# A two-block transformer kernel: the Silu of a condition vector moved, three coefficient rows made at another point of the program

## The chip, the cores and the metric

The kernel runs on one core of a Trainium2 chip. Its time is the device time of one execution in microseconds (us); the number compared is the median of several executions. The engines of the core are PE (matrix multiply; PEld loads its weights), DVE (element-wise work on vectors), ACT (functions, copies, casts), POOL (here it only sets constants and issues transfers) and SP (it only issues transfers).

## What is computed

An activation of 256 rows by 1024 columns passes through two blocks. The first block is one mLSTM mixer (an attention-like recurrence with 4 heads, forward and backward in time) and a gated feed-forward with a convolution. The second has two layers, each of feed-forward, mixer, feed-forward; the mixers are a gated linear attention (GLA) and a latent attention (MLA). Every sub-layer is modulated by vectors that come out of a condition vector:

```
mod = silu(c) @ w_mod + b_mod
sh1, sc1, ga1, sh2, sc2, ga2 = split(mod, 6)
hx = modulate(x, g_mix, sh1, sc1)
y  = mlstm_mixer(hx, ...)
x  = x + ga1 * y
hx = modulate(x, g_ffn, sh2, sc2)
x  = x + ga2 * conv_glu(hx, ...)
```

The second block does the same with its own condition vector `c_2`. A vector such as `ga1` multiplies the mixer's output column by column, so with the 256 rows on the partitions it is wanted as a *row*: 1024 numbers, the same on all 128 partitions.

## The kernel before

Activations lie in two tiles of 128 rows. Every weight is streamed from DRAM by SP in pieces of 128 x 1024 (512 KB) through a few `raw` buffers; ACT casts a piece to a high part (`whi`, L236), DVE subtracts to get the low part (`wlo`, L237), and each product is three matmuls (L250 to L252). "A projection" below is one of these matmuls of 512 columns.

The products of a condition vector with its weights are done on DVE while the other engines work on the main path: for each 128 outputs one piece of weight is loaded to `raw` and one instruction of DVE (`ttr`, L256) multiplies it with the condition row and sums. They stand in a list, `bg_queue`; `site()` takes as many from its front as a table says (`FILL`), and `need(keys)` takes from it until the named ones are done. The condition row is 128 x 1024, `c1` for the first block and `c2` for the second, which share one buffer (tag `crow`), so `c2` can't be written before the last `ttr` with `c1` has read it. `c2()` makes the row where it is first asked for: SP sends `c_2` from DRAM to all partitions (L158) and ACT applies Silu to all 128 x 1024 (L159).

`row_of(v)` turns a vector that lies as 128 x 8 into a row: PE transposes it (`rowp`, L389) into the one PSUM buffer of tag `tr`, ACT copies it out (`s8`, L391), POOL writes it to DRAM (`d<-s`, L393) and sends it back to all partitions (`row<-d`, L395). The same PSUM buffer `tr` holds `mp` of the mLSTM attention.

The mLSTM mixer first makes q, k, v and the output gate o (`as_proj`, four groups of 1024 columns; the gate's Sigmoid is L696). Then `attend(t, h)` runs for 2 row tiles x 4 heads: PE makes the scores (L706) and spreads the gate sums over the partitions (`mp`, L710), DVE and ACT turn them into weights (L716, Exp at L719 and L720, products at L722 to L725), PE multiplies them with the values (L733), and DVE and ACT normalise (L735 to L744). Then `wo_proj` is the output projection; its last step multiplies with the row `ga1` (L761). GLA and MLA have the same shape, and their last step multiplies with a row in `post2` (L921).

The order of instructions on each engine is the scheduler's: it goes by the order of the program, except that `urgent(offset)` lifts work by that many places. Attention runs under `urgent(300)` for the first tile and `urgent(2000)` for the second, so its instructions are put ahead of things written earlier, if what they need is there.

Of the kernel before, what the change touches and what calls it, by code (L numbers as in the profile page):

```python
# [7 lines left out]
F32 = mybir.dt.float32  # L8
# [3 lines left out]
AF = mybir.ActivationFunctionType  # L12
# [4 lines left out]
D = 1024  # L17
# [93 lines left out]
def kernel(ctx: ExitStack, tc: tile.TileContext, a: dict, out: bass.AP):  # L111
    nc = tc.nc
    V, S, T, G = nc.vector, nc.scalar, nc.tensor, nc.gpsimd
# [9 lines left out]
    row_p = pool("row", 2)  # L123
# [3 lines left out]
    sm = pool("sm", 4)  # L127
    dr = pool("dr", 2, space=bass.MemoryType.DRAM)
# [24 lines left out]
    def col(name, i=0, n=None):  # L153
        off, tot = COLS[name]
        return cols[:, off + i:off + i + (tot if n is None else n)]

    def load_act_row(src, dst):
        nc.sync.dma_start(out=dst, in_=src.partition_broadcast(128))  # L158
        S.activation(out=dst, in_=dst, func=AF.Silu)  # L159

    cc = ar.tile([128, D], F32, name="cc", tag="Q")
    c1 = row_p.tile([128, D], F32, name="c1", tag="crow", bufs=1)
# [106 lines left out]
    def site():  # L269
        bg(filler.pop(0))  # L270

    def need(*keys):
        while not done.issuperset(keys):
            bg()
# [17 lines left out]
    def scale1(dst, g):  # L292
        V.scalar_tensor_tensor(out=dst, in0=dst, scalar=1.0, in1=g, op0=ALU.add, op1=ALU.mult)
# [92 lines left out]
    def row_of(c):  # L386

        p = ps_tr.tile([8, 128], F32, name="rowp", tag="tr")
        T.transpose(p, c, ident)  # L389
        s8 = sm.tile([8, 128], F32, name="s8", tag="s8", bufs=2)  # L390
        S.copy(s8, p)  # L391
        d = dr.tile([8, 128], F32, name="d", tag="d")
        G.dma_start(out=d, in_=s8)  # L393
        r = row_p.tile([128, D], F32, name="row", tag="row")
        G.dma_start(out=r, in_=d.rearrange("a b -> (a b)").partition_broadcast(128))  # L395
        return r

    def row_load(src):
        r = row_p.tile([128, D], F32, name="row", tag="row")
        G.dma_start(out=r[:, :src.shape[-1]], in_=src.partition_broadcast(128))  # L400
        return r
# [40 lines left out]

    vec2 = []

    def c2():
        if not vec2:
            v = row_p.tile([128, D], F32, name="c2", tag="crow", bufs=1)
            load_act_row(a["c_2"], v)
            vec2.append(v)
        return vec2[0]  # L450

    for i, fin in ((2, None), (3, None), (4, "g_ffn"), (5, None)):
        dst = mod1[:, i, :]
# [153 lines left out]
    def mlstm():  # L607
# [94 lines left out]
        def attend(t, h):  # L702
# [40 lines left out]
            dst = so[:, t, h * 256:h * 256 + 256]  # L743
            V.scalar_tensor_tensor(out=dst, in0=hs, scalar=r, in1=dst, op0=ALU.mult, op1=ALU.mult)  # L744

        for t in range(2):
            with urgent(2000 if t else 300):
                for h in range(H):
                    attend(t, h)
                t_hilo(so[:, t, :], t)  # L750
            site()

    mlstm()
    need(("m", 2), ("m", 3), ("m", 4))
    ga1 = row_of(mod1[:, 2, :])

    def fin_mix(t, acc):
        y = wk.tile([128, D], F32, name="y", tag="xn")
# [250 lines left out]
    def gla():  # L1009
# [8 lines left out]
        rt = scratch(1).rearrange("p (t n) -> p t n", t=2)  # L1018
        gout = hp.tile([128, 256], F32, name="gout", tag="gout", bufs=1)
        G.dma_start(out=gout, in_=a["gl_gout"].partition_broadcast(128))  # L1020
        units, got = {}, {}

        def vr(i, t):
# [60 lines left out]
        with urgent():  # L1084
# [20 lines left out]
            for t in range(2):  # L1105
# [34 lines left out]
                    dst = rt[:, t, h * 256:h * 256 + 256]  # L1140
                    V.scalar_tensor_tensor(out=dst, in0=po, scalar=r, in1=dst, op0=ALU.mult, op1=ALU.mult)
                t_hilo(rt[:, t, :], t)
        need(5, 6, 7)
        coef = row_of(mod2[:, 5, :])

        def fin(t, acc):
            post2(coef, t, acc)
# [101 lines left out]
    def mla_mix():  # L1249
        scale = 192.0 ** -0.5  # L1250
        msk = hp.tile([128, 256], F32, name="amsk", tag="gout", bufs=1)
        G.dma_start(out=msk, in_=a["amask"])
        gq = row_load(a["mla_gq"])
        def attend(t, h):
            rp = slice((h % 2) * 64, (h % 2) * 64 + 64)
            n = 128 * (t + 1)
# [76 lines left out]
        for step in MLA_STEPS:  # L1333
            steps[step[0]](*[int(x) for x in step[1:]])
            site()
        need(14, 15, 16)
        coef = row_of(mod2[:, 14, :])

        def fin(t, acc):
            post2(coef, t, acc)  # L1340
# [162 lines left out]
```

## Time and profile before

| | us |
|---|---|
| median of 3 executions | 1430.35 |
| lowest, highest | 1429.79, 1434.51 |
| the profiled execution, its own time | 1434.38 |
| its span in the trace | 1432.6 |

The span is what the trace shows from the first to the last instruction; 1.8 us of the profiled execution's time lie outside it. Its mean granted clock of PE is 0.986 of full speed. In the page, busy time is the time in which an engine has an instruction running; a row of the timeline has, in brackets, how long the engine had been idle before the instruction, and what it was waiting for.

### The profile page before, as it was taken

How to read it: one execution, taken by the hardware profiler on the slowest of the kernel's cores; microseconds unless marked ns; L12 is line 12 of the kernel's file. 1: busy time of each engine (PE TensorE's matmuls, PEld its weight loads, DVE VectorE, ACT ScalarE, POOL GpSimd, SP SyncE). 2: the span in 40 equal slices, each digit the busy share in tenths (PEclk: the TensorE clock that was granted, in tenths of full speed). 3: DMA queues.
4: the chain of work that ended last, by engine and by line, in shares of the span. 5: the costliest groups of instructions: out<-in, count | busy, mean ns of one | idle time of the engine just before them, and what ended most of it. 6: DMA issues, size and time to landing. Idle time of an engine off the chain costs nothing.

```text
span 1432.6 us, 22526 instructions
## 1 busy us (share of the span) xinstructions
PE 1380.0 (96%) x8425; PEld 1204.0 (84%) x8425; DVE 1113.9 (78%) x2115; ACT 720.5 (50%) x1188; POOL 18.2 (1%) x42
## 2 busy tenths in 40 slices
PE   6999999999989999999999999999999999899997
PEld 6978877899978999878678999879999776789996
DVE  6887788898688888689788888698878786756563
ACT  4634764545354545566454545554554666644451
POOL 1000000000000000000000000000000000000000
PEclk8999999999999999999999999999999999999999
DMA  8576446797528999568548999469889472366750
GB/s 330 203 265 234 162 151 234 264 323 272 184 96 290 336 340 345 196 222 290 187 154 289 341 335 344 147 202 334 317 310 333 138 253 80 121 198 205 276 170 30
DMA packets 94943, 340.24 MB, mean 238 GB/s; under 512 B 10928, under 2 KB 11248, under 8 KB 94832
## 3 DMA queue, kind: packets, MB, share of 16 engines
q1 hardware_dynamic: 92736, 332.47, 65.6%
q0 software_dynamic: 2096, 6.33, 1.5%
q8 instruction: 66, 1.08, 0.3%
q14 instruction: 45, 0.37, 0.1%
HBM read 337.67 MB, written 1.08 MB: 236 GB/s over the span
## 4 chain that ended last, share of the span: by engine, by line
PE 70%; DVE 11%; DMA 10%; ACT 4%; issue 3%; SPq 0%; DVEq 0%; ACTq 0%; POOLq 0%
PE mm L250 12%; PE mm L252 11%; PE mm L251 11%; PE acc L252 8%; PE acc L250 8%; PE acc L251 8%; DMA raw<-in_cond_w_dram 3%; DVE wlo L237 3%; DVE gjunk L256 2%; PE acc L733 2%; ACT whi L236 1%; ACT ajunk L324 1%; PE pt L347 1%; PE pg L556 1%; DMA row<-d 1%
## 5 line engine op out<-in xcount | busy, mean ns | idle before, releaser
L237 DVE TENSOR_TENSOR wlo<-raw,whi 128x1024 fp32r<-128x1024 f32 (+1 forms) x385 | 462.5, 1207 | 109.6 <-ACT whi L236 106.7
L236 ACT CAST whi<-raw 128x1024 fp32r<-128x1024 f32 (+1 forms) x385 | 395.7, 1038 | 277.1 <-PE mm L251 79.5
L250 PE MATMUL mm<-u_hi,whi 128*128 128x256 f32 x1384 | 388.5, 281 | 0.2 <-DVE hf L831 0.2
L251 PE MATMUL mm<-u_lo,whi 128*128 128x256 f32 x1384 | 386.6, 279 | 0.0
L252 PE MATMUL mm<-u_hi,wlo 128*128 128x256 f32 x1384 | 386.5, 279 | 0.0
L250 PEld LDWEIGHTS mm<-u_hi,whi 128*128 128x128 f32 x1384 | 260.0, 188 | 4.4 <-DVE hf L831 0.6
L251 PEld LDWEIGHTS mm<-u_lo,whi 128*128 128x128 f32 x1384 | 259.3, 187 | 3.3
L252 PEld LDWEIGHTS mm<-u_hi,wlo 128*128 128x128 f32 x1384 | 260.1, 188 | 0.0
L256 DVE CUSTOM_DVE_ANT_0 gjunk<-raw,c 128x1024 bf16<-128x1024 f32 x192 | 234.3, 1221 | 24.1 <-DMA raw<-in_cond_w_dram 16.5
L250 PE MATMUL acc<-whi,hh 128*128 128x512 f32 x388 | 153.6, 398 | 4.5 <-ACT hh L245 4.5
L252 PE MATMUL acc<-whi,hl 128*128 128x512 f32 x388 | 153.3, 397 | 0.3 <-DVE hl L246 0.3
L251 PE MATMUL acc<-wlo,hh 128*128 128x512 f32 x388 | 152.5, 393 | 0.5 <-DVE wlo L237 0.5
L252 PEld LDWEIGHTS acc<-whi,hl 128*128 128x128 f32 x388 | 73.4, 189 | 17.4 <-DVE hl L246 0.7
L250 PEld LDWEIGHTS acc<-whi,hh 128*128 128x128 f32 x388 | 72.9, 188 | 17.5 <-ACT hh L245 5.0
L252 PE MATMUL acc<-whi,u_lo 128*128 128x512 f32 (+1 forms) x216 | 86.7, 403 | 0.5 <-DVE u_lo L246 0.5
L250 PE MATMUL acc<-whi,u_hi 128*128 128x512 f32 (+1 forms) x216 | 86.5, 401 | 0.0
L251 PE MATMUL acc<-wlo,u_hi 128*128 128x512 f32 (+1 forms) x216 | 86.4, 400 | 0.0
L251 PEld LDWEIGHTS acc<-wlo,hh 128*128 128x128 f32 x388 | 73.2, 189 | 14.2 <-DVE wlo L237 1.3
L251 PE MATMUL mm<-wlo,u_hi 128*128 128x512 f32 x144 | 57.3, 398 | 0.0
L250 PE MATMUL mm<-whi,u_hi 128*128 128x512 f32 x144 | 57.2, 397 | 0.0
L252 PE MATMUL mm<-whi,u_lo 128*128 128x512 f32 x144 | 57.0, 397 | 0.0
L946 ACT ACTIVATE sg<-mm 128x256 f32<-128x256 f32 x64 | 24.3, 380 | 59.6 <-PE mm L252 59.5
(734 smaller groups left out, 1998.6 us busy)
## 6 DMA issues: line engine op xcount, KB each, us to landing
raw<-in_cond_w_dram SPq DMA_DIRECT2D x144, 512.0 KB, 5.2
raw<-in_gu_ws_dram SPq DMA_DIRECT2D x128, 512.0 KB, 5.0
raw<-in_dn_dram SPq DMA_DIRECT2D x88, 512.0 KB, 4.9
raw<-in_gu_dram SPq DMA_DIRECT2D x48, 512.0 KB, 4.3
raw<-in_w_mod_dram SPq DMA_DIRECT2D x32, 512.0 KB, 4.3
raw<-in_f_down_dram SPq DMA_DIRECT2D x22, 512.0 KB, 4.6
raw<-in_f_gate_dram SPq DMA_DIRECT2D x18, 512.0 KB, 4.9
raw<-in_a_vo_dram SPq DMA_DIRECT2D x16, 512.0 KB, 5.1
```

The lines of the kernel that those rows point to most:

```text
L236: o1 = S.copy(hi[:, :n], r[:, :n])
L237: o2 = V.tensor_tensor(out=lo[:, :n], in0=r[:, :n], in1=hi[:, :n].bitcast(F32), op=ALU.subtract)
L250: T.matmul(ps, lhsT=lh, rhs=rh, start=first, stop=False)
L251: T.matmul(ps, lhsT=lh, rhs=rl, start=False, stop=False)
L252: T.matmul(ps, lhsT=ll, rhs=rh, start=False, stop=last)
L256: return V.tensor_tensor_reduce(out=junk, in0=r, in1=vec, scale=1.0, scalar=0.0, op0=ALU.mult, op1=ALU.add, accum_out=dst)
L324: mark["ms"] = S.activation(out=junk[:, :src.shape[-1]], in_=src, func=AF.Square, scale=float(2 * width) ** -0.5, accum_out=dst)
L347: T.transpose(pt[:, k, :], src[:, (h * 4 + k) * 128:(h * 4 + k + 1) * 128], ident)
L556: o = T.matmul(pg, lhsT=wsc[:, k * 128:k * 128 + 128], rhs=ccol[:, k, :], start=(k == 0), stop=(k == 7))
L733: T.matmul(np_[:, 0:257], lhsT=w[:, d, s, :], rhs=vt[s][:, h, :], start=(i == 0), stop=(i == len(tiles) - 1))
L946: S.activation(out=sg, in_=ps[:, 0:256], func=AF.Silu)
```

## The change

Two things are done.

1. The condition row `c2`. `load_act_row` and the instruction of ACT on 128 x 1024 go. `c2_ahead`, called in the mLSTM mixer before its attention, loads `c_2` as 8 x 128 by POOL, applies Silu to 8 x 128, and writes it to DRAM by POOL. `c2_row`, which runs as the last step of the product m5 (the last that reads `c1`), sends it from DRAM to the buffer `crow` by POOL.
2. The rows. `row_of` is called ahead of the attention instead of behind it in the mLSTM mixer (`ga1`), GLA and MLA, with a `need` for its vector ahead of it.

```diff
-    def load_act_row(src, dst):
-        nc.sync.dma_start(out=dst, in_=src.partition_broadcast(128))
-        S.activation(out=dst, in_=dst, func=AF.Silu)
...
+    def c2_ahead():
+        v = sm.tile([8, 128], F32, name="c2s", tag="s8", bufs=2)
+        G.dma_start(out=v, in_=a["c_2"].rearrange("(a b) -> a b", a=8))
+        S.activation(out=v, in_=v, func=AF.Silu)
+        d = dr.tile([8, 128], F32, name="c2d", tag="c2d", bufs=1)
+        G.dma_start(out=d, in_=v)
+        vec2.append(d)
+
+    def c2_row():
+        v = row_p.tile([128, D], F32, name="c2", tag="crow", bufs=1)
+        G.dma_start(out=v, in_=vec2[0].rearrange("a b -> (a b)").partition_broadcast(128))
+        vec2.append(v)
+
     def c2():
-        if not vec2:
-            v = row_p.tile([128, D], F32, name="c2", tag="crow", bufs=1)
-            load_act_row(a["c_2"], v)
-            vec2.append(v)
-        return vec2[0]
+        return vec2[1]
...
+        c2_ahead()
+        need(("m", 2))
+        row = row_of(mod1[:, 2, :])
         for t in range(2):
             with urgent(2000 if t else 300):
...
-    mlstm()
-    need(("m", 2), ("m", 3), ("m", 4))
-    ga1 = row_of(mod1[:, 2, :])
+        return row
+    ga1 = mlstm()
+    need(("m", 3), ("m", 4))
...
+        need(5)
+        coef = row_of(mod2[:, 5, :])
...
-        need(5, 6, 7)
-        coef = row_of(mod2[:, 5, :])
+        need(6, 7)
...
+        need(14)
+        coef = row_of(mod2[:, 14, :])
...
-        need(14, 15, 16)
-        coef = row_of(mod2[:, 14, :])
+        need(15, 16)
```

Each line number moves by a few places in the changed kernel (the matmuls L250 to L252 are its L246 to L248, L706, L710, L733 are its L713, L717, L740, and `rowp` L389 is its L385).

The scheduler's order moves too. PE before, inside the mLSTM attention: the first matmuls with the values (L733) stand after 11 projections into the sum `acc_1101`, and the other projections follow among them; from there to `rowp`, row 714, attention and projections alternate.

```order
514 L252 MATMUL acc_1101<-whi,u_lo 128x512
515 L250 MATMUL acc_1101<-whi,u_hi 128x512
516 L251 MATMUL acc_1101<-wlo,u_hi 128x512
517 L733 MATMUL acc_1443<-vt_910,scr_1419 128x257 x2
518 L710 MATMUL mp<-gm,ident 128x128 x2
519 L733 MATMUL acc_1443<-vt_911,scr_1419 128x257
520 L733 MATMUL acc_1449<-vt_910,scr_1419 128x257 x2
521 L733 MATMUL acc_1449<-vt_911,scr_1419 128x257 x2
522 L706 MATMUL mm<-qT,kT 128x128 x4
```

PE after, the same attention. The 144 projections of rows 504 to 647 stand in one piece ahead of it, and the last of them are the first two rows here.

```order
646 L247 MATMUL acc_1392<-wlo,u_hi 128x512
647 L248 MATMUL acc_1392<-whi,u_lo 128x512
648 L385 MATMUL rowp<-ident,mod_117 8x128
649 L717 MATMUL mp<-gm,ident 128x128 x2
650 L740 MATMUL acc_1456<-vt_910,scr_1419 128x257 x2
651 L717 MATMUL mp<-gm,ident 128x128 x2
652 L740 MATMUL acc_1456<-vt_911,scr_1419 128x257
653 L740 MATMUL acc_1462<-vt_910,scr_1419 128x257 x2
654 L740 MATMUL acc_1462<-vt_911,scr_1419 128x257 x2
655 L713 MATMUL mm<-qT,kT 128x128 x4
656 L717 MATMUL mp<-gm,ident 128x128 x2
657 L740 MATMUL acc_1510<-vt_910,scr_1419 128x257 x2
```

Behind `rowp` all eight `attend` follow one another, with 22 projections (of the output projection) among them up to row 721, and `mp` of the first head stands behind `rowp`, with which it shares its PSUM buffer. On ACT the Exp and Sigmoid that alternated now stand apart, which takes 6 table loads out.

DVE before, in the feed-forward of the first block (`hf` is a piece of its hidden layer, `hl` the low part of it): the first `ttr` with `c2`, here called `c_2574`, is row 464.

```order
455 L831 TENSOR_TENSOR hf<-g,mm 128x256
456 L819 TENSOR_SCALAR g<-mm,cols 128x256
457 L246 TENSOR_TENSOR hl<-hf,hh 128x256
458 L820 SCALAR_TENSOR_TENSOR g<-mm,cols,g 128x192
459 L237 TENSOR_TENSOR wlo<-raw,whi 128x1024
460 L821 SCALAR_TENSOR_TENSOR g<-mm,cols,g 128x192
461 L819 TENSOR_SCALAR g<-mm,cols 128x256
462 L831 TENSOR_TENSOR hf<-g,mm 128x256
463 L820 SCALAR_TENSOR_TENSOR g<-mm,cols,g 128x192
464 L256 ISA gjunk,mod_118<-raw,c_2574 128x1024
465 L256 ISA mod_118 128x1
466 L246 TENSOR_TENSOR hl<-hf,hh 128x256
```

DVE after, the same place; `c2` is called `c_2543`.

```order
450 L831 SCALAR_TENSOR_TENSOR g<-mm,cols,g 128x192
451 L252 ISA gjunk,mod_118<-raw,c_2543 128x1024
452 L252 ISA mod_118 128x1
453 L841 TENSOR_TENSOR hf<-g,mm 128x256
454 L829 TENSOR_SCALAR g<-mm,cols 128x256
455 L252 ISA gjunk,mod_118<-raw,c_2543 128x1024
456 L252 ISA mod_118 128x1
457 L242 TENSOR_TENSOR hl<-hf,hh 128x256
458 L830 SCALAR_TENSOR_TENSOR g<-mm,cols,g 128x192
```

The first two `ttr` with the new row now stand ahead of `hf` and of `hl`. SP's order only loses the transfer of `c_2`; on POOL the two small transfers of `c2_ahead` and the broadcast of `c2` come in, the last between the rows `ga1` and that of the feed-forward.

PE before, end of the MLA mixer (L1276 is the last product of its attention): `rowp` stands behind it.

```order
6513 L250 MATMUL acc_12804<-whi,u_hi 128x512
6514 L251 MATMUL acc_12804<-wlo,u_hi 128x512
6515 L1276 MATMUL acc_12744<-pT,scr_12117 128x128 x2
6516 L389 MATMUL rowp<-ident,mod_118 8x128
6517 L252 MATMUL acc_12804<-whi,u_lo 128x512
6518 L250 MATMUL acc_12917<-wA,u_hi 128x512
```

PE after, start of the MLA mixer; the rows ahead of `rowp` are the last of the feed-forward before it.

```order
6184 L247 MATMUL acc_9730<-wlo,hh 128x512
6185 L248 MATMUL acc_9730<-whi,hl 128x512
6186 L385 MATMUL rowp<-ident,mod_118 8x128
6187 L246 MATMUL mm<-c_hl,wU_11259 128x256
6188 L247 MATMUL mm<-c_hl,wU_11259 128x256
6189 L343 MATMUL pt<-ident,xn 128x128 x4
```

`rowp` has moved by 330 rows, past the whole of the attention. In GLA `rowp` moves in the same way, from row 3625 to row 3182.

## Rows read from the trace of the kernel before

**Rows 1.** The page's line of busy time, share of the span, instructions, by engine.

```profile
PE 1380.0 (96%) x8425; PEld 1204.0 (84%) x8425; DVE 1113.9 (78%) x2115; ACT 720.5 (50%) x1188; POOL 18.2 (1%) x42
```

**Rows 2.** Windows: busy us (instructions) of PE, PEld, DVE, ACT, POOL; PEclk, DMA, GB/s.

```profile
180.00:200.00 20.00, 20.00 (x95) 16.62 (x94) 17.80 (x65) 16.10 (x31) 1.09 (x3) 1.00 0.44 146
...
240.00:260.00 20.00, 15.44 (x103) 13.68 (x102) 14.81 (x31) 9.12 (x14) 1.06 (x2) 0.91 0.70 240
...
1220.00:1240.00 20.00, 16.05 (x62) 12.52 (x61) 15.39 (x44) 13.20 (x28) 0.00 (x0) 0.83 0.14 55
```

**Rows 3.** Timeline inside the mLSTM attention: start, us, engine, line, operation, [idle before <- releaser].

```profile
127.86 1.05 PE L706 MATMUL mm<-qT,kT 128*128 128x128 f32 x8
...
129.54 0.71 PE L710 MATMUL mp<-gm,ident 64*128 64x128 f32 x4
...
130.18 3.30 PE L733 MATMUL acc<-vt,scr 128*128 128x257 f32 x14
...
132.40 1.23 DVE L256 CUSTOM_DVE_ANT_0 gjunk<-raw,c 128x1024 bf16<-128x1024 f32 x1
...
135.54 0.48 DVE L741 SCALAR_TENSOR_TENSOR hs<-acc,dn,hs 128x256 f32<-128x256 f32 x1 [0.85 <-ACT hs L740]
...
135.86 1.03 PE L733 MATMUL acc<-vt,scr 128*128 128x257 f32 x4
```

**Rows 4.** ACT groups by line, 123 to 196 us: busy us, mean ns | idle before.

```profile
L236 ACT CAST whi<-raw 128x1024 fp32r<-128x1024 f32 x13 | 13.6, 1048 | 3.9 <-PE acc L252 3.9
L719 ACT ACTIVATE scr<-mp,gc 128x128 f32<-128x128 f32 x38 | 11.7, 366 | 11.7 <-DVE scr L716 7.8 <-DVE dn L737 2.1 <-DVE r L309 1.6
...
L719 ACT ACT_TABLE_LOAD x4 | 5.1, 1283 | 1.4 <-DVE scr L716 1.2
...
L696 ACT ACTIVATE scr<-acc 128x512 f32<-128x512 f32 x4 | 2.4, 597 | 4.1 <-PE acc L252 4.0
```

**Rows 5.** Timeline behind the mLSTM attention, PE.

```profile
212.20 0.63 PE L347 MATMUL pt<-ident,xn 128*128 128x128 f32 x4 [1.61 <-DVE xn L370]
```

**Rows 6.** Timeline where the second condition vector arrives: SP, ACT, PE.

```profile
243.16 0.33 SPq L158 DMA_DIRECT2D c<-in_c_dram  x1
...
250.69 1.06 ACT L159 ACTIVATE c<-c 128x1024 f32<-128x1024 f32 x1 [4.74 <-DMA c<-in_c_dram]
251.66 0.39 ACT L245 CAST hh<-hf 128x256 fp32r<-128x256 f32 x1
...
252.10 0.50 PE L250 MATMUL acc<-whi,hh 128*128 128x512 f32 x1 [4.22 <-ACT hh L245]
```

**Rows 7.** The tile `row`: its broadcast transfers from issue to landing.

```profile
DMA to landing us min/median/max: 4.7/6.6/8.3
```

**Rows 8.** Timeline at the end of the MLA mixer, ACT, PE and DVE.

```profile
1212.38 0.25 ACT L391 COPY s<-rowp 8x128 f32<-8x128 f32 x1
...
1217.91 0.40 PE L252 MATMUL acc<-whi,u_lo 128*128 128x512 f32 x1
...
1221.94 1.29 DVE L921 TENSOR_TENSOR y<-acc,row 128x512 f32<-128x512 f32 x2 [5.00 <-DMA row<-d]
```

**Rows 9.** PE alone behind it.

```profile
1231.21 0.66 PE L347 MATMUL pt<-ident,xn 128*128 128x128 f32 x4 [2.43 <-DVE xn L370]
...
1238.83 0.63 PE L251 MATMUL mm<-wB,u_hi 128*128 128x512 f32 x1
1239.25 0.53 PE L252 MATMUL mm<-wB,u_lo 128*128 128x512 f32 x1
1239.62 0.39 PE L250 MATMUL mm<-wB,u_hi 128*128 128x512 f32 x1
1239.85 0.39 PE L251 MATMUL mm<-wB,u_hi 128*128 128x512 f32 x1
```

**Rows 10.** PE at the start of the GLA mixer.

```profile
622.47 0.66 PE L347 MATMUL pt<-ident,xn 128*128 128x128 f32 x4 [0.81 <-DVE xn L370]
```

**Rows 11.** Timeline at the start of the kernel, PE.

```profile
14.55 3.55 PE L556 MATMUL pg<-ccol,wsc 128*128 128x2 f32 x16 [5.29 <-DMA wsc<-in_w_sc_dram]
```

More of the change, by code (lines that the diff above doesn't have):

```diff
@@ L443 @@
     vec2 = []
-    def c2():
-        if not vec2:
-            v = row_p.tile([128, D], F32, name="c2", tag="crow", bufs=1)
-            load_act_row(a["c_2"], v)
-            vec2.append(v)
-        return vec2[0]
-    for i, fin in ((2, None), (3, None), (4, "g_ffn"), (5, None)):
+    def c2_ahead():
[9 more added lines that the diff above has]
+        vec2.append(v)
+    def c2():
+        return vec2[1]
+    for i in range(2, 6):
         dst = mod1[:, i, :]
         q_gemv(("m", i), a["w_mod"][i - 2], lambda: c1, dst, col("b_mod", i * 8, 8),
-               (lambda dst=dst: scale1(dst, col("g_ffn"))) if fin else None)
+               (lambda dst=dst: scale1(dst, col("g_ffn"))) if i == 4 else c2_row if i == 5 else None)
     def ng(l, s, w):
```

## The prediction

> **What bounds the kernel now.** I read the page's busy times first. PE is busy for 1380.0 of 1432.6 us [rows 1]; all its idle time is 52.6 us, so a change that adds no work to PE can win only from that, and from stretches in which the clock granted to PE is halved. The windows say where both lie. Inside the mLSTM attention there is nothing to win: PE is busy 20.00 of 20 us at full clock, while DVE has 17.80 and ACT 16.10 [rows 2]. Two of the windows that the change touches have a hole: 240 to 260 us (PE 15.44, clock 0.91) and 1220 to 1240 us (PE 16.05, clock 0.83). Then I read the timeline of each engine around the moved instructions, for who waits for whom.
>
> **mLSTM: what is removed is hidden, what is added is not.** Before, `row_of` stood behind the attention. The wait that this leaves at the end is PE's 1.61 us for the normalised next input [rows 5]. With `ga1` made early that chain starts sooner and 30 projections lie beside it, so I count -1.6 (bounds -1.6 and 0).
>
> The price is the order. Before, heads and projections alternate, so while a head's weights go through ACT and DVE, PE has projections to do. After, the order shows all 144 projections first, then `rowp`, and only then `mp` of the first head, since both use the one PSUM buffer. So at that point PE has only the first head to wait for. On ACT, counted from the end of the last projection: the Sigmoid of the gate (0.60) [rows 4], the copy of `rowp` out of PSUM (0.25) [rows 8], and only then may `mp` be written; then, in ACT's queue, a cast of a weight piece (1.05) and a table load (1.28) ahead of the Exps [rows 4]. That makes 3.2 us; two Exps (0.37 each, overlapped) and a product on DVE make it some 4.3 us until PE can start on the values. In it PE has `rowp` and `mp` (0.2 and 0.4), so it is idle for about 3.7 us. If the cast and the table load were done earlier, 0.85 would be left; that is the lower bound.
>
> Such a hole has a second price. In 240 to 260 us PE stood for 4.22 us [rows 6] and the window's clock is 0.91 [rows 2], one of its two levels being 2.4 GHz and the other half of it: (1 - 0.91) x 20 = 1.8 us lost at the most, some of it in the idle time. I take 1.5 for the like hole here (bounds 0 and 1.8).
>
> Then the steady state. A head costs PE 8 matmuls of scores, 4 of `mp` and 14 with the values [rows 3]: less the overlaps 0.85 + 0.64 + 3.05, about 4.5 us. Two heads in a row began their values at 130.18 and 135.86, so a head took 5.68 us before, but in it DVE had a `ttr` of 1.23 and was idle for 0.85 [rows 3]; its own work for a head is therefore about 5.68 - 1.23 - 0.85 = 3.6 us. After the change no `ttr` stands among the first seven heads on DVE. The bounds are a head at PE's own 4.5 us (no stall) and a head at the 5.68 seen (1.2 of stall). DVE's work at 3.6 being under PE's, I take a value near the first, 0.2 of stall for each of 8 heads: +1.6 (bounds 0 and 9.6).
>
> Sum for mLSTM: 3.7 + 1.5 + 1.6 - 1.6 = +5.2; bounds 0.85 - 1.6 = -0.7 and 3.7 + 1.8 + 9.6 = +15.1. The table loads that go (6 x 1.28 = 7.7 us of ACT) are counted at nothing: PE was full beside them [rows 2]. The `ttr` that `need` puts ahead lie on DVE beside the 144 projections; if they delayed a `wlo` there, PE would wait for it, and that is in the upper bound.
>
> **c2: the stall changes its owner.** Before, SP issued the row at 243.16, it landed 7.5 us later, ACT took 1.06 for Silu with the cast `hh` queued behind it, and PE restarted at 252.10 after 4.22 idle [rows 6]. What made it wait is the buffer: `c1` is read until 243.05, and the new transfer goes to the same buffer, so it can't be issued earlier either. What changes is that Silu is gone (-1.06) and that the first `ttr` with `c2` now stands ahead of `hf` on DVE: landing + `ttr` 1.23 [rows 3] + `hf` (about 0.4, as `hh`) + `hh` 0.39 [rows 6] = landing + 2.0. The trace has no transfer of this one's kind but the `row` broadcasts from DRAM by POOL, 4.7, 6.6 and 8.3 us from issue to landing [rows 7]. From 243.2 that gives a restart at 249.9, 251.8 or 253.5, against 252.10: -2.2, -0.3 or +1.4. I take the median. `hl` stands behind a second `ttr`, and PE asks for it some 1.3 us after its restart: +0.3. Sum 0, bounds -4.0 (the first, with 1.8 of clock) and +1.7.
>
> The rows put a 512 KB broadcast at 4.7 us or more. The Trainium skill, DMA: Bandwidth & Descriptors, "Anatomy of one DMA", fits a transfer issued by POOL as about 2.0 us plus its bytes at 436 GB/s; that would be an estimate of 3.2 us here and a restart at 248.4, a gain of 3.7 and the clock besides. No broadcast of this size in the trace was as short, beside weights streaming on SP's queue.
>
> The Silu of 8 x 128 at the start stands on ACT between two activations, where the critical thing is the weights for the gates, for which PE waits until 14.55 [rows 11]: 0, or up to +1 if its own small transfer is late. The three small transfers on POOL pass nothing that is waited for: 0.
>
> **GLA.** `ga` was never late there (the trace has no wait of L921 for the row in it). After, the copy out of PSUM stands ahead of an activation of the chain for which PE waited 0.81 us [rows 10]: +0.2, bounds 0 and +1.
>
> **MLA: a real wait goes.** `rowp` was copied out at 1212.38, the output projection of the first tile ended at 1217.91 + 0.40, but DVE could start L921 only at 1221.94, when the row landed, 5.00 us idle [rows 8]. So the chain to the next input comes up to 3.6 us earlier. PE waited 2.43 us for that chain's end [rows 9]; that goes. Behind it matmuls ran 0.42 us apart (1238.83 to 1239.25) and then 0.23 (1239.62 to 1239.85) [rows 9], so at half clock; 11 of them cost 11 x 0.19 = 2.1 us. I take half of that, 1.1, since a later wait in the chain (the second tile's) stays. Sum -3.5, bounds -4.5 and -1.5. Next late is that second tile.
>
> **Sum.** 5.2 + 0 + 0.2 - 3.5 = +1.9 us. The profiled execution took 1434.38, so 1436.3 for an execution like it. That one lies 4.0 above the median of the three, 1430.35; for the median I subtract that: 1432.2.
>
> **The rivals.**
> A, faster. The attention's start is covered: the cast and the table load are done before the last projection, so only 0.85 of idle is left and the clock stays up, +0.9 with the heads as above; `c2` lands soon, after 4.7 us or less, and PE's clock doesn't fall there, -4.0; MLA gives all, -4.5. Together -7.6: 1422.8. For it: ACT has been idle before each such step in the trace. Against it: the order puts the cast and the table load behind the copy, and the median of landing is 6.6. The skill's fit above points to this side.
> B, slower. The head's own chain (`mp`, Exps, products, values, then `mp` of the next) decides and not PE's work, so each head takes 5.68 us as before, without projections to fill it: 9.6 + 3.7 + 1.8, MLA -3.5: +11.6, 1442.0. It decides from a head of about 5.0 us on. For it: one buffer for `mp`. Against it: DVE's 3.6 us of work.
> C, `c2` lands late (8.3 us and both `ttr` ahead): +1.7, so 1433.9.
> That the change saves what it names, and nothing follows from it since the same waits stand elsewhere, is part of my forecast.
>
> **How the numbers follow.** Forecast 0.50 (its own range 1428 to 1437), A 0.18, B 0.20, C 0.12. About 0.3% (4.3 us) is what a measurement of this kernel tells from no change. Of the forecast 0.02 is faster, 0.40 the same, 0.08 slower; of A 0.15 and 0.03; B is slower; of C 0.08 the same, 0.04 slower. That makes 0.17 faster, 0.51 the same, 0.32 slower. The range reaches to most of A and of B: 1424 to 1441.
>
> **What would show it.** In the trace after: PE idle of 3 to 4 us right ahead of the first L740, with a clock under 1 in that window; L740 of successive heads some 4.7 us apart (B: 5.7); DVE idle for the DMA of `c2` ahead of a `ttr`, and PE idle by about 4 us there again; no wait of L921 for a row in MLA and `pt` without idle time. I am wrong if PE is full through the mLSTM attention, or if the hole near 250 us has closed.

## The result and the profile after

The changed kernel took 1442.87 us (median of 6 runs, 1441.69 to 1444.01), the kernel before, run in turn with it, 1434.76 (6 runs, 1429.79 to 1437.96). The ratio is 1.006 with a 95% interval of 1.004 to 1.0081, so about +8.6 us (5.7 to 11.6). The forecast was +1.9 and "the same"; the time lies above the range. The profiled execution has a span of 1440.9 us, 8.3 more than before. Three executions of later kernels (one of `c2_sp`, two of `c2_own`), which took 1518 to 4111 us, are left out of all ratios.

The first row is the page's line of busy time after; it answers to [rows 1].

```profile
PE 1385.6 (96%) x8425; PEld 1207.4 (84%) x8425; DVE 1115.7 (77%) x2115; ACT 712.7 (49%) x1182; POOL 19.7 (1%) x45
```

The count of PE's instructions is the same, and they were busy for 5.6 us longer; the six table loads of ACT are gone. So part of the loss is the same matmuls at a lower clock. The windows after (busy us and instructions of PE, PEld, DVE, ACT, POOL; then PEclk, DMA, GB/s) answer to [rows 2]; from 240 us on the kernel lies 6 to 12 us later. In the kernel before, PE was busy for 20.00 of 20 us at a clock of 1.00 in both windows from 140 to 180.

```profile
140.00:160.00 20.00, 16.31 (x68) 12.48 (x66) 13.41 (x18) 12.17 (x18) 1.06 (x2) 0.91 0.76 269
160.00:180.00 20.00, 19.47 (x93) 16.18 (x93) 12.93 (x62) 9.80 (x32) 0.00 (x0) 0.83 0.10 32
...
240.00:260.00 20.00, 15.57 (x95) 13.32 (x94) 14.57 (x26) 8.79 (x11) 1.04 (x2) 0.97 0.85 308
1220.00:1240.00 20.00, 20.00 (x93) 15.70 (x92) 11.34 (x29) 9.32 (x21) 0.00 (x0) 1.00 0.30 105
```

A new hole stands at 140 to 160 with a reduced clock in it and behind it; the hole near 250 is still there; the one near 1230 has closed.

**The new hole.** This is the timeline after, from the last projection to the first product with the values (start, us, engine, line, operation, [idle before <- releaser]); it answers to [rows 3].

```profile
153.75 0.60 ACT L703 ACTIVATE scr<-acc 128x512 f32<-128x512 f32 x1 [0.34 <-PE acc L248]
154.25 0.24 ACT L387 COPY s<-rowp 8x128 f32<-8x128 f32 x1
154.39 1.04 ACT L232 CAST whi<-raw 128x1024 fp32r<-128x1024 f32 x1
154.53 0.71 PE L717 MATMUL mp<-gm,ident 64*128 64x128 f32 x4 [0.71 <-ACT s L387]
...
155.45 1.28 ACT L726 ACT_TABLE_LOAD   x1
156.74 0.62 ACT L726 ACTIVATE scr<-mp,gc 128x128 f32<-128x128 f32 x2
...
157.67 0.41 DVE L729 TENSOR_TENSOR scr<-scr,mm 128x256 f32<-128x256 f32 x1
...
158.23 2.05 PE L740 MATMUL acc<-vt,scr 128*128 128x257 f32 x4 [2.98 <-DVE scr L729]
...
178.60 1.13 PE L713 MATMUL mm<-qT,kT 128*128 128x128 f32 x8 [0.53 <-DVE dn L746]
...
218.73 0.62 PE L343 MATMUL pt<-ident,xn 128*128 128x128 f32 x4
```

Read from the top: Sigmoid, copy of `rowp`, cast, table load, Exp, product, and only then PE. PE waits 0.71 for the buffer that `rowp` held and 2.98 for the first head. Behind it the heads follow with a single wait of 0.53, and the last row has no wait any more, where [rows 5] had 1.61.

**The condition row.** The timeline after at the place of [rows 6].

```profile
249.23 0.53 POOL L453 DMA_DIRECT2D c<-c2d  x1 [51.73 <-DVE mod L252]
...
256.12 1.23 DVE L252 CUSTOM_DVE_ANT_0 gjunk<-raw,c 128x1024 bf16<-128x1024 f32 x1 [4.40 <-DMA c<-c2d]
257.27 0.41 DVE L841 TENSOR_TENSOR hf<-g,mm 128x256 f32<-128x256 f32 x1
...
257.72 0.41 ACT L241 CAST hh<-hf 128x256 fp32r<-128x256 f32 x1 [5.55 <-DVE hf L841]
257.83 0.63 PE L819 MATMUL mm<-ident,lead 128*128 128x128 f32 x4 [4.08 <-DVE hf L841]
258.21 0.48 PE L246 MATMUL acc<-whi,hh 128*128 128x512 f32 x1
```

The transfer takes 6.9 us; DVE stands for 4.40 in front of a `ttr`, `hf` is queued behind it, and PE stands for 4.08.

**GLA and MLA.** The timeline after at the start of GLA (answers to [rows 10]), and behind it the end of MLA (to [rows 8, 9]).

```profile
623.98 0.53 POOL L391 DMA_DIRECT2D row<-d  x1 [1.55 <-DVE ss L330]
624.92 7.14 SPq L178 DMA_DIRECT2D raw<-in_cond_w_dram  x2
630.47 1.23 DVE L252 CUSTOM_DVE_ANT_0 gjunk<-raw,c 128x1024 bf16<-128x1024 f32 x1 [1.14 <-DMA raw<-in_cond_w_dram]
633.25 0.66 PE L343 MATMUL pt<-ident,xn 128*128 128x128 f32 x4 [2.04 <-DVE xn L366]
...
1231.61 1.39 DVE L931 TENSOR_TENSOR y<-acc,row 128x512 f32<-128x512 f32 x2 [2.81 <-PE acc L248]
1240.92 0.66 PE L343 MATMUL pt<-ident,xn 128*128 128x128 f32 x4 [0.28 <-DVE xn L366]
```

In GLA, PE's wait has grown from 0.81 to 2.04. In MLA, L931 waits for the product and no longer for the row; PE's wait of 2.43 is 0.28.

**Where the time went.** The table gives, for the same PE instruction, its start in a kernel's trace minus its start in the trace of before (head of the column: the start in before, us). A difference between two columns is what that stretch cost more than before. The lower kernels are the experiments told of next; each row is one execution.

| kernel | 240.72 | 256.54 | 412.01 | 605.99 | 622.47 | 964.37 | 1188.33 | 1246.54 | 1408.08 |
|---|---|---|---|---|---|---|---|---|---|
| after | +6.3 | +6.4 | +8.7 | +9.4 | +10.8 | +11.2 | +12.0 | +7.7 | +8.8 |
| ml_only | +6.1 | +3.5 | +6.3 | +6.4 | +6.4 | +7.0 | +9.0 | +9.0 | +9.0 |
| c2_only | +2.6 | +3.8 | +5.4 | +5.5 | +5.7 | +4.3 | +8.0 | +7.6 | +7.6 |
| gla_only | -1.0 | -2.2 | -2.9 | -2.2 | -0.5 | 0.0 | -0.3 | -0.7 | -0.7 |
| mla_only | +0.1 | -2.1 | -0.5 | -0.4 | -0.4 | -1.2 | +0.4 | -4.0 | -3.1 |
| no_ml | +1.6 | +2.9 | +3.0 | +3.7 | +5.7 | +6.4 | +9.9 | +5.5 | +6.3 |
| ml_tc | +3.5 | +2.3 | +3.1 | +3.7 | +3.9 | +3.9 | +5.1 | +5.0 | +5.0 |
| c2_own | +1.4 | -2.3 | +0.1 | +0.1 | +0.1 | -0.4 | +3.7 | -0.5 | +0.4 |
| c2_sp_b | +0.5 | -0.5 | +2.9 | +2.6 | +2.7 | +2.9 | +5.7 | +4.4 | +4.4 |
| gla_late | -1.2 | -2.9 | -3.3 | -2.3 | -2.0 | -1.4 | +4.1 | +4.7 | +4.7 |
| best2 | -0.1 | -2.8 | -1.9 | -1.1 | -1.1 | -1.5 | -1.0 | -5.3 | -4.5 |

Two columns are sharp: from 605.99 to 622.47 every kernel with the early GLA row loses 1.4 to 2.0 and every other at most 0.3; from 1188.33 to 1246.54 `after`, `mla_only`, `no_ml` and `best2` gain 4.3 to 4.4 (`c2_own` 4.2, for a reason told below). Others scatter: from 964.37 to 1188.33, where but for `c2_own` only the place of one row differs, the cost is between -0.3 and +5.5. Part of that is the clock: in the 10 us from 1120 it is 0.83 in `c2_only`, 0.71 in `no_ml` and 0.75 in `gla_late`, and 1.00 in before. A single trace therefore tells a stretch's wait, but not the kernel's time to better than some us; for that the medians are taken.

### The profile page after: what moved, and what is told of

Same layout as the page of the kernel before. It is cut to its first block, busy times and chain, and to the rows that moved or that the text cites. A ratio compares the mean times of both kernels' runs of the same rounds, so it can differ in the third digit from the quotient of the medians.

```text
span 1440.9 us, 22527 instructions
## 1 busy us (share of the span) xinstructions
PE 1385.6 (96%) x8425; PEld 1207.4 (84%) x8425; DVE 1115.7 (77%) x2115; ACT 712.7 (49%) x1182; POOL 19.7 (1%) x45
## 4 chain that ended last, share of the span: by engine, by line
PE 66%; DVE 11%; issue 9%; DMA 8%; ACT 5%; SPq 0%; POOL 0%; DVEq 0%; ACTq 0%; POOLq 0%
PE mm L246 12%; PE mm L248 11%; PE mm L247 11%; PE acc L248 8%; PE acc L246 8%; PE acc L247 8%; DMA raw<-in_cond_w_dram 3%; DVE wlo L233 3%; DVE gjunk L252 2%; ACT whi L232 1%; ACT ajunk L320 1%; DMA raw<-in_gu_ws_dram 1%; PE pg L563 1%; DMA wsc<-in_w_sc_dram 1%; PE pt L343 1%
## 5 line engine op out<-in xcount | busy, mean ns | idle before, releaser
L246 PE MATMUL mm<-u_hi,whi 128*128 128x256 f32 x1384 | 388.6, 281 | 0.1
L248 PE MATMUL mm<-u_hi,wlo 128*128 128x256 f32 x1384 | 386.6, 279 | 0.0
L246 PEld LDWEIGHTS mm<-u_hi,whi 128*128 128x128 f32 x1384 | 260.0, 188 | 4.1 <-DVE hf L841 0.4
L248 PEld LDWEIGHTS mm<-u_hi,wlo 128*128 128x128 f32 x1384 | 260.2, 188 | 0.0
L252 DVE CUSTOM_DVE_ANT_0 gjunk<-raw,c 128x1024 bf16<-128x1024 f32 x192 | 234.3, 1220 | 30.6 <-DMA raw<-in_cond_w_dram 20.6
L248 PE MATMUL acc<-whi,hl 128*128 128x512 f32 x388 | 153.2, 396 | 1.1 <-DVE hl L242 1.1
L246 PE MATMUL acc<-whi,hh 128*128 128x512 f32 x388 | 153.7, 398 | 0.6 <-ACT hh L241 0.6
L248 PEld LDWEIGHTS acc<-whi,hl 128*128 128x128 f32 x388 | 73.4, 189 | 18.2 <-DVE hl L242 1.6
L248 PE MATMUL acc<-whi,u_lo 128*128 128x512 f32 (+1 forms) x216 | 86.2, 400 | 0.4 <-DVE u_lo L242 0.4
L246 PE MATMUL acc<-whi,u_hi 128*128 128x512 f32 (+1 forms) x216 | 86.0, 399 | 0.0
L246 PEld LDWEIGHTS acc<-whi,hh 128*128 128x128 f32 x388 | 73.1, 189 | 13.3 <-ACT hh L241 0.8
L246 PE MATMUL mm<-whi,u_hi 128*128 128x512 f32 x144 | 57.2, 397 | 0.0
L248 PE MATMUL mm<-whi,u_lo 128*128 128x512 f32 x144 | 57.1, 397 | 0.0
```

Of the source, the lines that this page charges most:

```text
L246: T.matmul(ps, lhsT=lh, rhs=rh, start=first, stop=False)
L248: T.matmul(ps, lhsT=ll, rhs=rh, start=False, stop=last)
L252: return V.tensor_tensor_reduce(out=junk, in0=r, in1=vec, scale=1.0, scalar=0.0, op0=ALU.mult, op1=ALU.add, accum_out=dst)
```

## The experiments

### Each part alone

`c2_only` has the condition row of the change and nothing else, `ml_only`, `gla_only` and `mla_only` one early row each. For MLA it is

```diff
+        need(14)
+        coef = row_of(mod2[:, 14, :])
         ...
-        need(14, 15, 16)
-        coef = row_of(mod2[:, 14, :])
+        need(15, 16)
```

and alike for the others.

> Only the condition row c2 is made the new way; the three coefficient rows stay behind their attention. Theory (the prediction's step on c2, as the trace after bears it out): the same wait of some 4 us stands near 250 us, now on DVE ahead of the first ttr with c2, and behind it weights of the feed-forward come later, since ttr and weights share the raw buffers: +2 us, between 0 and +3. Rival: nothing is wrong with c2 by itself and the +2.4 us seen between 250 and 310 us of the trace after come from the shifted list of background products (need takes some earlier): 0 or up to -1. Second rival: without Silu on 128 x 1024 and with the row soon, a gain of 2 to 4 us.

> Only the row ga1 of the mLSTM mixer is made ahead of its attention. Theory: the transpose takes the one PSUM buffer of mp, so the attention is held until the 144 projections are done; PE idle of 3.5 to 4 us before the first product with the values, a clock under 1 behind it, and +6 us in all at the end of the mixer (the trace after has +6.1 there). Rival: the +6 needs the other parts too (POOL's small transfers, the new SP order), and alone it is below +3.

> Only the coefficient row of the GLA mixer is made ahead of its attention. Theory: in the trace after PE lost 2 to 2.7 us between 609 and 730 us, so alone it costs +1.5 to +3 us. Rival (as predicted): +0.2, not to be told from 0, and the loss there comes from something that another part moved.

> Only the coefficient row of the MLA mixer is made ahead of its attention. Theory: the wait of DVE for the row (5.0 us) and PE's 2.43 us behind it go, and part of the half clock: -3 to -5 us, so faster than the kernel before. Rival: some 1.3 us are given back ahead of and inside the mixer (the trace after lost 1.9 us between 1044 and 1150 us), which leaves -2 to -3.

Measured, as ratio to before with its interval, and the us that it makes:

| kernel | ratio | interval | us |
|---|---|---|---|
| ml_only | 1.005 | 1.0032 to 1.0067 | +7.2 |
| c2_only | 1.0031 | 1.0013 to 1.005 | +4.4 |
| gla_only | 1.0005 | 0.9987 to 1.0023 | +0.7 |
| mla_only | 0.9972 | 0.9953 to 0.9992 | -4.0 |

They add to +8.3, and the whole change measures +8.6, so these four runs give no sign that the parts meet each other. The sum is uncertain by about 5 us to either side, and `no_ml` below fits it less well. `ml_only` shows the same hole, 0.71 and 2.98 us, and the same clocks behind it (0.91 and 0.84). PE in `c2_only`, same columns as above:

```profile
254.34 1.09 PE L817 MATMUL mm<-ident,lead 128*128 128x128 f32 x4 [4.20 <-DVE hf L839]
260.38 0.66 PE L817 MATMUL mm<-ident,lead 128*128 128x128 f32 x4 [1.12 <-DVE hf L839]
```

`mla_only` has the old way at that place, its row going out by SP (L158) and Silu on ACT:

```profile
242.99 0.33 SPq L158 DMA_DIRECT2D c<-in_c_dram  x1
249.85 1.06 ACT L159 ACTIVATE c<-c 128x1024 f32<-128x1024 f32 x1 [4.06 <-DMA c<-in_c_dram]
251.25 0.50 PE L250 MATMUL acc<-whi,hh 128*128 128x512 f32 x1 [3.08 <-ACT hh L245]
```

So the old way costs PE 3.08 here, not the 4.22 of [rows 6], and the new one 4.20 and another 1.12. The landing is what differs from before's profile: 6.8 us here, 7.5 there.

### The mLSTM hole: the vector's time, or the shared buffer

`ml_need` only asks for the vector ahead of the attention and makes the row where it was; `ml_tc` is `ml_only` with `rowp` in another PSUM buffer:

```diff
-        row = row_of(mod1[:, 2, :])
+        row = row_of(mod1[:, 2, :], "tc")
```

> The kernel before with only need of m2 called ahead of the mLSTM attention; the row ga1 is made behind it as before. Theory (the transpose in mp's buffer makes the loss of the mLSTM part): within 1.5 us of the kernel before. Rival (the products of the condition vector, taken earlier, make it or a part of it): +3 us or more, as much as the run with the transpose in the other buffer lost.

> As the run with only the row ga1 made ahead of the mLSTM attention, but its transpose goes to the other small PSUM buffer (tag tc), which mp doesn't use. In the scheduler's order heads and projections alternate again as in the kernel before. Theory (the one PSUM buffer makes the loss): no hole before the first product with the values, PE full from 120 to 200 us, and the time within 2 us of the kernel before, perhaps -1 to -2 since the row comes sooner. Rival (the early need of m2, which puts products of the condition vector ahead, makes the loss): +4 to +7 us again.

`ml_need` measures 1.0003 (0.999 to 1.0017): no cost of the `ttr` that are put ahead is seen (+0.4 us, between -1.4 and +2.4). `ml_tc` measures 1.0027 (1.0016 to 1.0038), +3.9 against +7.2. In its trace the attention and the projections alternate again and the hole ahead of the first head is gone. What is left are two other waits of PE, later in the attention:

```profile
187.58 3.30 PE L733 MATMUL acc<-vt,scr 128*128 128x257 f32 x14 [1.71 <-ACT hs L740]
192.44 1.14 PE L733 MATMUL acc<-vt,scr 128*128 128x257 f32 x4 [1.56 <-ACT hs L740]
```

That the hole goes with the shared buffer is shown, and that it isn't the whole price too, since +3.9 (2.3 to 5.4) stays without it. In the trace 1.5 us of what is left lie ahead of the attention, near 90 us, where the clock is 0.83 for 10 us and 1.00 in before. Why `hs` is late was not tried.

### The condition row: the transfer's issuer, the queue on DVE, the buffer

Two edits to `c2_only`, and two to the kernel before. `c2_small` adds the small load, Silu and write to the kernel before, and nobody reads what they make. `c2_sp` is `c2_only` with the broadcast issued on SP instead of POOL. `c2_own` is `c2_only` with a buffer of its own for `c2`, so that the transfer needn't wait until `c1` has been read: the program asks for it a product earlier, and in the trace POOL issues it already at 14.75 us. For room, `cq` of MLA shares the buffer of `qs`. `cq_qs`, told of below, has only this second half of `c2_own`. First `c2_sp`, then `c2_own`.

```diff
-        G.dma_start(out=v, in_=vec2[0].rearrange("a b -> (a b)").partition_broadcast(128))
+        nc.sync.dma_start(out=v, in_=vec2[0].rearrange("a b -> (a b)").partition_broadcast(128))
```

```diff
-        v = row_p.tile([128, D], F32, name="c2", tag="crow", bufs=1)
+        v = row_p.tile([128, D], F32, name="c2", tag="crow2", bufs=1)
...
-               (lambda dst=dst: scale1(dst, col("g_ffn"))) if i == 4 else c2_row if i == 5 else None)
+               (lambda dst=dst: (scale1(dst, col("g_ffn")), c2_row())) if i == 4 else None)
...
-                 cn = wk.tile([128, 384], F32, name="cq", tag="cq", bufs=1)
+                 cn = wk.tile([128, 384], F32, name="cq", tag="qs", bufs=1)
```

> The kernel before with only the first half of the c2 change added: c_2 is loaded as 8 x 128, goes through Silu and is written to DRAM by POOL, and nobody reads it; the row c2 is made the old way. Theory (what the new way loses, it loses where the row is used, near 250 us): within 1 us of the kernel before. Rival (the small transfers and the small Silu at the start, or the places in the order that they shift, make the loss): +3 to +4 us, as all kernels with the new way have shown.

> Only the condition row c2 is made the new way, but its broadcast from DRAM is issued by SP, at the place in SP's order where the old transfer stood, not by POOL; on DVE hf then stands ahead of the first ttr with c2. Theory (ttr ahead of hf and the shifted weights make the loss of the new way): PE restarts sooner near 250 us, and the time is within 1.5 us of the kernel before or up to 2 us better, so 3 to 5 us better than the same change with POOL. Rival (the small transfers, or waits of another kind, make the loss): as slow as with POOL, +3 to +5 us.

> Only the condition row c2 is made the new way, and it gets a buffer of its own (the room comes from two buffers of the MLA mixer, cq and qs, made one), and its broadcast is issued as the last step of the product m4, long before c1 has been read for the last time. Theory (the stall near 250 us is the wait for c1's buffer, whoever issues the transfer): the idle time of 4.2 us there and its half clock are gone, -3 to -6 us against the kernel before. Rival: something else is late there then, weights that share the raw buffers above all, and the gain is under 1.5 us.

`c2_small`: 1.001 (0.9998 to 1.0023), so +1.4 us, between -0.3 and +3.3: no loss is shown, but that the small transfers make a part of the +4.4 isn't excluded. `c2_sp`: 1.0026 (1.0014 to 1.0039), +3.7 us, as its rival has it. Its trace is taken from one more execution of the same kernel, `c2_sp_b` (1438.23 us):

> The same program as the run with the broadcast of c2 issued by SP, looked at once more for its trace (the trace of that run was disturbed). Theory (with the new way PE's restart near 250 us is late by the ttr that stands ahead of hf): here hf stands ahead of it, so PE is idle for 2.4 to 3.6 us there, as in the kernels with the old way, and no second wait for hf of 1.1 us follows. Rival (the new way is late for another reason): 4 us and the second wait again.

```profile
246.27 0.42 DVE L839 TENSOR_TENSOR hf<-g,mm 128x256 f32<-128x256 f32 x1 [0.49 <-ACT g L830]
250.60 1.23 DVE L252 CUSTOM_DVE_ANT_0 gjunk<-raw,c 128x1024 bf16<-128x1024 f32 x1 [3.91 <-DMA c<-c2d]
252.22 0.50 PE L248 MATMUL acc<-whi,hl 128*128 128x512 f32 x1 [3.08 <-DVE hl L242]
271.67 0.39 PE L246 MATMUL mm<-u_hi,whi 128*128 128x256 f32 x1 [2.63 <-DVE hf L839]
```

Here `hf` stands ahead of the `ttr`, and PE loses 3.08 instead of 4.20 plus 1.12. But a wait of 2.63 for a later `hf` follows, the table shows +3.4 from 256.54 to 412.01, and the median has hardly gained on `c2_only`. So the order on DVE explains the wait at 254 and not the kernel's time.

`c2_own`: 1.003 (1.0015 to 1.0045), +4.3 us (2.2 to 6.5) where a gain of 3 to 6 was expected. Its PE rows of that place show that the stall of 4 us can be removed:

```profile
254.23 0.66 PE L817 MATMUL mm<-ident,lead 128*128 128x128 f32 x4 [1.68 <-DVE hf L839]
264.33 0.63 PE L817 MATMUL mm<-ident,lead 128*128 128x128 f32 x4 [1.00 <-DVE hf L839]
269.05 0.39 PE L246 MATMUL mm<-u_hi,whi 128*128 128x256 f32 x1 [0.89 <-DVE hf L839]
```

Three smaller waits for `hf` take its place, and of the 3.7 us gained up to 256.54 the table shows 2.4 lost again by 412.01. The shared buffer in MLA has a price too, which `cq_qs`, the second of the two edits alone on the kernel before, measures:

> The kernel before with only the two MLA buffers cq and qs made one, as the run with c2 in its own buffer needed for room. Theory (the trace of that run lost 3.6 us inside the MLA mixer, between 1170 and 1182 us, and gained near 250): +3 to +5 us, so that c2 in a buffer of its own is by itself about even or up to 1 us better. Rival: 0 to +1, and c2 loses 4 us even with its own buffer.

1.0016 (0.9997 to 1.0034). Its trace loses 3.9 us between 1167 and 1182 and gains 4.2 up to 1246, since in its order the row of MLA lands in time without the change: L921 waits for the product and not for the row, and PE's wait for `xn` behind it is 0.27, where [rows 9] have 2.43. Taking 2.3 us off, `c2_own` would stand at about +2, but the intervals of the two don't exclude 0.

### GLA: a transfer in the way of a weight

`gla_late` asks for the vector and makes the row behind the mixer's projections in the program, just ahead of its attention, instead of ahead of the projections.

> Only the GLA row is made ahead of its attention, but later than in the changed kernel: behind the projections in the program, by which the scheduler puts its transpose just ahead of the transposes of the mixer's second input tile, so that its 512 KB broadcast starts after the weights that the chain before those transposes waits for. Theory (in the changed kernel the broadcast takes DMA time from a weight piece, and the ttr that waits for that piece stands inside the chain of the norm on DVE): that ttr doesn't wait, PE waits for xn by 0.8 us as in the kernel before, not 2.0 to 2.3, and the time is within 1.5 us of the kernel before. Rival (the copy of the transpose on ACT, or the POOL work, makes the loss): PE waits for xn by 1.5 us or more.

It measures 1.0002 (0.9984 to 1.002), `gla_only` 1.0005 (0.9987 to 1.0023); the times don't tell them apart, the traces do. First `gla_only`: the row is issued ahead of the weight that the `ttr` in the norm's chain wants. Behind it a window of 4 us, columns as above.

```profile
612.47 0.55 POOL L395 DMA_DIRECT2D row<-d  x1 [1.62 <-DVE ss L334]
613.34 7.41 SPq L182 DMA_DIRECT2D raw<-in_cond_w_dram  x2
619.16 1.23 DVE L256 CUSTOM_DVE_ANT_0 gjunk<-raw,c 128x1024 bf16<-128x1024 f32 x1 [1.40 <-DMA raw<-in_cond_w_dram]
621.94 0.66 PE L347 MATMUL pt<-ident,xn 128*128 128x128 f32 x4 [2.30 <-DVE xn L370]
```

```profile
614.00:618.00 4.00, 4.00 (x19) 3.27 (x18) 2.26 (x8) 2.67 (x6) 0.00 (x0) 1.00 0.94 319
```

And `gla_late`, the same two views:

```profile
613.20 6.10 SPq L182 DMA_DIRECT2D raw<-in_cond_w_dram  x2
617.71 1.23 DVE L256 CUSTOM_DVE_ANT_0 gjunk<-raw,c 128x1024 bf16<-128x1024 f32 x1 [0.20 <-DMA raw<-in_cond_w_dram]
620.49 0.66 PE L347 MATMUL pt<-ident,xn 128*128 128x128 f32 x4 [0.99 <-DVE xn L370]
623.37 0.55 POOL L395 DMA_DIRECT2D row<-d  x1 [1.62 <-DMA d<-s]
```

```profile
614.00:618.00 4.00, 4.00 (x19) 3.28 (x18) 2.46 (x8) 2.92 (x7) 0.00 (x0) 1.00 0.60 184
```

With the row out of the way the DMA engines are busy 0.60 of the window instead of 0.94, the `ttr` starts 4.51 us after the issue of its weight piece (613.20 to 617.71) instead of 5.82 (613.34 to 619.16), and waits 0.20 instead of 1.40. The copy of `rowp` on ACT has moved with the row, so the two kernels alone don't separate it; but the wait of the `ttr` is for the DMA, and it makes 1.20 of the 2.30 - 0.99 = 1.31 us that PE waits less. The Trainium skill, DMA: Bandwidth & Descriptors, "Issuing engines are not separate DMA queues", says that transfers of all issuing engines run on the same 16 DMA engines and interleave. The traces agree: a broadcast issued by POOL delays a weight issued by SP, here by 1.40 - 0.20 = 1.2 us.

### Combinations

`no_ml` is the change without the mLSTM row; `best1` is `c2_own` with the MLA row; `best2` is `gla_late` with the MLA row.

> The changed kernel without its mLSTM part: c2 the new way, GLA and MLA rows ahead. Theory (the parts add: +4.4, +0.7 and -4.0 by their own runs): +1 us, between -2 and +3, so that the mLSTM row accounts for nearly all of the +8.6 us. Rival (they don't add, MLA's gain is lost when work is late ahead of it): +4 or more.

> c2 in a buffer of its own as in the run before this one, and the MLA row made ahead of its attention. Theory: the two gains add, -4 of MLA and -3 to -6 of c2: -7 to -10 us, about 0.6%. Rival: they don't add (MLA's two buffers made one cost there what the row gains): -4 or less.

> The later GLA row and the MLA row ahead of its attention, nothing else of the change. Theory: MLA's gain alone, -3 to -5 us against the kernel before, as the run with the MLA row alone. Rival: the gain of that run was chance, and this one is within 1.5 us.

`no_ml`: 1.0038 (1.0024 to 1.0052), +5.5, above the +3 that was the most expected. The parts add to 4.4 + 0.7 - 4.0 = +1.1, but each of the three has about 2.7 us of uncertainty to either side, together 4.6, so the sum doesn't exclude +5.5. `best1`: 1.0038 (1.0022 to 1.0053), +5.5 where a gain of 7 to 10 was expected; between 1167 and 1182 its trace loses 6.9 us with the shared buffer, more than the MLA row gives back. `c2_own` loses 3.6 there; the clock from 1170 to 1190 is 0.66 in `best1` and 0.91 in `c2_own`. `best2`: 0.9989 (0.9971 to 1.0006), with the gain of MLA in its trace; its interval still holds no change. The fastest kernel is `mla_only`, and the only one that beats both kernels beyond its interval. Its window at that place, and PE in it, which has lost the wait and the reduced clock of [rows 2, 9]:

```profile
1220.00:1240.00 20.00, 18.22 (x81) 13.99 (x80) 17.40 (x48) 15.46 (x30) 0.00 (x0) 1.00 0.15 53
```

```profile
1229.25 0.66 PE L347 MATMUL pt<-ident,xn 128*128 128x128 f32 x4 [0.28 <-DVE xn L370]
```

## Why the prediction was wrong

Each term against the kernel that has only that part:

| term | forecast | bounds | measured alone (interval) |
|---|---|---|---|
| mLSTM | +5.2 | -0.7 to +15.1 | +7.2 (4.6 to 9.6) |
| c2 | 0 | -4.0 to +1.7 | +4.4 (1.9 to 7.2) |
| GLA | +0.2 | 0 to +1 | +0.7 (-1.9 to 3.3) |
| MLA | -3.5 | -4.5 to -1.5 | -4.0 (-6.7 to -1.1) |
| sum | +1.9 | | +8.6 (5.7 to 11.6) |

The miss of 8.6 - 1.9 = 6.7 us is 4.4 of c2, 2.0 of mLSTM, 0.5 of GLA, -0.5 of MLA, and 0.3 that the four parts don't hold.

**The step that failed is c2**: "I take the median. ... Sum 0, bounds -4.0 and +1.7". Its mechanism was right. After the change PE took up `hh` again at 258.21 (0.38 after it had begun the transposes ahead of it), 8.98 us from the issue, which is a landing of 6.9 and about the 2.0 of the prediction. What was wrong is what this was compared with. The 252.10 of [rows 6] comes from one execution in which the old transfer took 7.5 us. I set against it the median of other transfers, 6.6, and so credited the change with 0.9 us of a faster landing, which the transfer's way doesn't give: seven other traces with the old way (`gla_only`, `mla_only`, `ml_need`, `cq_qs`, `c2_small`, `gla_late`, `best2`) land in 6.1 to 6.9, with PE idle for 2.4 to 3.6, and the three with the new one in 6.8 to 6.9, with PE idle for 4.1 to 4.3. (`ml_only` and `ml_tc`, whose mLSTM stage was changed, lie in the ranges of the seven: 6.3 and 6.6, PE idle for 2.5 and 3.1.) From 240.72 to 256.54 the old way costs -1.5 on the mean of these seven, in the table's terms, the new one +0.9 on the mean of `after`, `c2_only` and `no_ml`. So the place costs +2.4: from landing to `hh` and PE's product with it are 2.1 instead of the 1.4 of [rows 6], since the `ttr` of 1.23 with `hf` behind it is dearer than the Silu of 1.06 that went, and in two of the three traces a second `hf` then comes 1.12 late, where I had put 0.3 for `hl`.

The other 2 us of the +4.4, whose interval of 1.9 to 7.2 leaves open whether there are so many, don't stand at this place. A part is clock. The span times one minus the mean granted clock is on the mean 21.6 us in the ten executions of `c2_only` and 18.9 in the 26 of before that were run in turn with them, 2.7 more (0.9 to 4.5). Two places of it are in the trace of `c2_only`; before has a clock of 1.00 in both windows.

```profile
90.00:100.00 10.00, 9.80 (x63) 9.29 (x64) 9.08 (x15) 1.76 (x5) 0.00 (x0) 0.83 0.80 258
1120.00:1130.00 10.00, 6.72 (x24) 5.09 (x23) 4.88 (x6) 2.85 (x5) 0.00 (x0) 0.83 0.67 229
```

That the new way brings these falls is not shown: `ml_tc` has the first and `gla_late` the second with the old way. `c2_sp` and `c2_own` changed the place and kept the loss, which speaks against a story of this one wait, and in `c2_own` no more is lost to the clock than in before (18.7 and 18.5). Where the rest goes is open, and the small transfers (`c2_small`) are not excluded.

The fit of the Trainium skill that stood beside this step (DMA: Bandwidth & Descriptors, "Anatomy of one DMA") gives the estimate of 3.2 us; no broadcast of `c2` in these traces landed under 6.1. The measurement decides. Plain weight pieces of the same 512 KB, issued by SP, land in 3.1 to 3.3 us where no other piece and no broadcast is beside them (before and `gla_late`, 608 to 624 us), so the estimate is near those and not near this broadcast beside streaming weights.

**mLSTM: mechanism right, the clock mis-sized.** Forecast were 3.7 of idle, 1.5 of clock, 1.6 of stalls, -1.6. The trace has 20 - 16.31 = 3.69 us of idle in the window of the hole, 0.53 of stalls behind it, and the wait of [rows 5] is gone. The stage costs +6.3 in the table, so the clock took some 6.3 - 3.7 - 0.5 + 1.6 = 3.7. The windows allow that: 0.91 and 0.83 are (0.09 + 0.17) x 20 = 5.2 us at most. The clocks of all executions say the same: their loss is on the mean 23.3 us in the six of `ml_only` and 18.9 in before, 4.4 more. I had counted one window, as at 250 in before; here two thirds of the loss (0.17 of 0.26) lie in the window behind. The stalls of the heads were 0.53, where I had put 1.6, so rival B, with its 9.6, fell. The sign that I had named for it did not decide: the first L740 of successive heads are 9.6, 4.9, 7.0, 6.8, 5.4, 4.8 and 4.5 us apart, not 4.7 throughout, since the lower clock and projections lie among them.

**GLA: wrong in cause, small in size.** I priced the copy on ACT (+0.2). At that place the traces lose 1.4 to 2.0, by the broadcast that delays a weight. The prediction asked who waits for the row, and not what lies on the DMA engines beside its transfer.

**MLA: right.** -3.5 forecast, -4.0 measured, -4.3 in the trace, by the wait and the clock named. PE's wait gave 2.43 - 0.28 = 2.15; the other 2.15 of the trace is clock, all of the 2.1 that I had halved.

**The start: right.** PE's first product for the gates began at 14.57, against 14.55 in [rows 11].

**The base.** The time missed by 10.7 us, of which the change explains 8.6 - 1.9 = 6.7. The rest is that I took the median of three, 1430.35, as the place of the kernel before; the six runs' median is 1434.76, close to the profiled execution's own 1434.38, from which I had subtracted 4.0. This is a second step that failed: without it the forecast of the time is 1436.3, and the rest of the miss is the change's.

**Rivals.** A fell with c2 and with the hole. B's time, 1442.0, is near the result, but for another reason: the heads did not decide. C had c2 at +1.7 by a landing of 8.3; the landing was 6.9, and the loss came from what stood in the queue and elsewhere.

## What to carry to other kernels

Before a wait is traded for another, take the old wait from several executions: one profile's 7.5 us landing was worth a credit that wasn't there. Moving a small piece of work ahead moves its buffers and its transfers with it: a transpose in a shared PSUM buffer made a barrier between the projections and the attention (+7.2, and +3.9 with another buffer), and a 512 KB broadcast delayed a weight piece on another queue (1.4 to 2.0 us in the traces, not to be told from 0 in the medians). Take the parts of such a change one by one: the one that removed a wait on the path (-4.0) was hidden under three that did not.

## What the runs showed that I had not expected

The clock does not fall in every execution that has the same hole. `c2_own` and `best1` differ only in MLA and have at 88 us nearly the same wait of PE. First `c2_own`, then `best1`: PE's wait in the timeline, and the window behind it.

```profile
88.89 0.33 PE L667 MATMUL mm<-ident,gm 64*128 64x64 f32 x2 [2.11 <-ACT gm L662]
```

```profile
90.00:100.00 10.00, 10.00 (x63) 9.45 (x62) 9.72 (x18) 1.61 (x4) 0.00 (x0) 0.83 0.86 304
```

```profile
88.67 0.34 PE L667 MATMUL mm<-ident,gm 64*128 64x64 f32 x2 [2.09 <-ACT gm L662]
```

```profile
90.00:100.00 10.00, 10.00 (x68) 9.17 (x67) 9.45 (x17) 1.56 (x4) 0.00 (x0) 1.00 0.82 289
```

One has a clock of 0.83, 1.7 us lost of 10, the other full clock. Over the whole span, the loss (span times one minus the mean granted clock) is 20.1 us in before, 24.5 in after, and 12.9 in `mla_only` and in `best2`; the last two have none of it near 250, 620 and 1230, where before lost 1.7, 1.7 and 3.4. A part of the scatter between executions of one kernel goes with it. The 114 executions of before that were run beside the experiments took 1428 to 1440 us; the 27 with a mean clock of at most 0.985 have a median of 1437.7, the 25 with at least 0.989 one of 1432.6. A change of a few us is therefore read from medians, and not from one execution.
